# Four weight loads a unit: the first issue at 0.4 instead of 0.1 slots, the distance 0.4 instead of 0.25

## The chip, the cores and the metric

The kernel runs on one core of a Trainium2 chip. The metric is the device time of one execution in microseconds (us); a kernel's time is the median of several executions. The profile is that of one execution, with its own time beside it.

## The reference

The kernel computes one encoder block for 2048 positions of width 1024. An RMS norm and one wide input projection give the queries, keys and values of 14 attention pieces, two gates' inputs and the merge gates. Attention looks at windows of neighbours (piece A, and three dilated groups of piece B with dilation 1, 4 and 16), the outputs are gated, projected and added to the input:

```python
h = rms_norm(x, norm_gain[layer])
proj = h @ w_in[layer]
qa, ka, va, qb, kb, vb, ga, gb, mg = jnp.split(proj, split_idx, axis=-1)
...
ya, _ = banded_attention(qa, ka, va, A_WINDOW, 1, rel_bias[:, :A_Q_HEADS], sink_a[layer])
ya = ya.reshape(bsz, S, A_WIDTH) * jax.nn.silu(ga)
...
    o, l = dilated_group(qb[:, :, g], kb[:, :, g], vb[:, :, g], window, dilation,
                         rel_bias[:, c0:c0 + B_HEADS_PER_GROUP])
...
yb = yb.reshape(bsz, S, B_WIDTH) * jax.nn.silu(gb)
br_a = ya @ w_branch_a[layer]
br_b = yb @ w_branch_b[layer]
...
merged = gates[:, :, 0] * br_a + gates[:, :, 1] * br_b
x = x + merged @ w_out[layer]
```

## The kernel before

**Numbers in two halves.** TensorE multiplies 16-bit numbers. Each float32 operand is therefore split into a high and a low f16 part, and a product takes three matmuls. The normed input stands in SBUF as `XH` and `XL`, transposed. The weights of a unit are loaded as float32 (`wraw`), multiplied by the norm's gain, squared and summed for a scale, and then split into `wh` and `wl`.

**Units and slots.** The attention pieces are 14 units (`UNITS`): piece A twice, and piece B in four head pairs times three groups `g`, in the order g = 1, 2, 0 for each head pair. A unit has eight slots, and a slot projects two blocks of 128 rows: two times 24 matmuls of line 709 with 384 columns. Slots can also hold "fills", products for the gates (line 333). After the units come four slots with fills alone, and then the gates, branches and output projection. The stretch with the units runs from about 70 to 1380 us.

**An order written by hand.** `at(t, f)` puts a step on a heap with its planned time in slots, and `until` emits what is due between two matmuls. This fixes the order of the instructions on each engine and on SyncE's DMA queue (SP). It fixes no time: on the chip each engine runs its list as fast as its waits allow. Planned times below are in slots from the first slot of a unit.

**What one slot makes.** The two projections are copied out of PSUM (`evac_qk`, `v_hi`, `v_lo`), queries and keys are normed and split (`square` to `swap`, on ScalarE, VectorE and GpSimd), and `turn` (line 794) issues two DMA transposes `kq<-spl` on SP. They are planned 1.118 slots behind the end of the slot's projections (`NORM`). An attention item then takes its logits (line 879, reads `kq`), and its probabilities are turned by a DMA transpose `pt<-p` (line 917) and multiplied with the values (line 928). Items are planned on a grid of half a slot for piece B: the first of a slot has its logits 2.887 slots behind the slot's start (`LS`), its `pt` 0.525 behind the logits and its values 1.829 behind them (`LAGS`, `LV`).

**The weights.** The tile `wraw` exists once. In unit u the weights of unit u + 1 are loaded, in four quarters of 384 KB (256 KB for the two weights behind the units). The loop below plans the four loads, the gains (`w_gain`, line 193, GpSimd), the squares, and the splits. In the last two slots of most units the same tile holds other weights, which are read for the last time by a split that is planned at 7.942. The steps of one `chain` keep their order among themselves.

```python
def w_load(u, parts=(0, 1, 2, 3)):
...
    for i in parts:
        nc.sync.dma_start(out=raw[:, 2 * i:2 * i + 2, :n], in_=src[:, 2 * i:2 * i + 2, :])
...
for u in range(NU + 1):
    t = 8 * u
    steps = [(t + W_STEP[0] + B_GAP[0] * i, w_load, u + 1, (i,)) for i in range(4)]
    for i in range(4):
        steps += [(t + W_STEP[2] - W_STEP[6] + W_STEP[3] * i, w_gain, u + 1, i),
```

With the values before, the loads are planned at 0.1, 0.35, 0.6 and 0.85 slots, and the gains at 1.558, 2.003, 2.448 and 2.893. The first eight slots prepare unit 1; the loads for unit 0 have planned times of their own. The loop has 15 rounds, so 60 loads.

Of the kernel before, what the change touches and what calls it, by code (L numbers as in the profile page):

```python
# [75 lines left out]
Y_DMA = (-0.097, 0.45, 0.55, 1.05, 1.13, 1.2, 1.25)  # L76
Y_MAX_DMA = (0.026, 1.4, 1.45)
GATE = (-0.123, -0.064, 0.329)
W_STEP = (0.1, 0.465, 1.9, 0.445, 4.197, 0.146, 0.342)
W_MAX = (3.762, 3.892)  # L80
G_PREP = (5.907, 6.882, 7.102, 7.671, 7.712, 7.812, 7.942)
N_PREP = (6.3, 7.15, 7.753)
B_GAP = (0.25, 0.138, 0.231)
Y_FREE = 0.15
Y_MAX = (0.026, 0.815, 0.839)
Y_MAX_A = (0.026, 0.88, 0.904)
# [37 lines left out]
def block_kernel(tc, x, w_units, w_gate, w_mrg, w_brn, w_out, w_bra, gain, qkg, sink, bias_a, bias_b, b_merge, out):  # L124
# [215 lines left out]
    def g_load(c, raw=None, parts=(0, 1)):  # L340
        if c not in gw:
            if raw is None:
                raw = sp0.tile([128, NCH, 128], F32, name="graw", bufs=2)[:]
            gw[c] = [raw]
        raw = gw[c][0]
        for i in parts:
            nc.sync.dma_start(out=raw[:, 4 * i:4 * i + 4, :], in_=w_gate[c][:, 4 * i:4 * i + 4, :])
# [76 lines left out]
    def at(t, f, *args):  # L424
        seq[0] += 1
        heapq.heappush(heap, (t, seq[0], f, args))
# [8 lines left out]
    def chain(steps):  # L435

        steps = sorted(steps, key=lambda e: e[0])
        done = [0]

        def go(k):  # L440
            if done[0] < k or steps[k][1](*steps[k][2:]) is False:
                at(now[0] + .04, go, k)
            else:
                done[0] = k + 1

        for k, e in enumerate(steps):
            at(e[0], go, k)
# [715 lines left out]
# [5 lines that stand above are left out]
                      (t + W_STEP[2] + W_STEP[3] * i, w_square, u + 1, i),  # L1168
                      (t + W_STEP[4] + W_STEP[3] * i, w_hi, u + 1, i),
                      (t + W_STEP[4] + W_STEP[5] + W_STEP[3] * i, w_lo, u + 1, i)]  # L1170
        chain(steps + [(t + d, f, u + 1) for d, f in zip(W_MAX, (w_sum, w_pow))])

    for c, u, slots in FILLS:
# [6 lines left out]
        for i in range(2):  # L1180
            at(t + G_PREP[0] + B_GAP[1] * i, lambda u=u, c=c, i=i: g_load(c, pre[u][0], (i,)))
        chain([(t + G_PREP[1] + .1 * i, g_gain, c, i) for i in range(2)]
              + [(t + d, f, c) for d, f in zip(G_PREP[2:], (g_square, g_sum, g_pow, g_hi, g_lo))])
    for k in range(8):
# [4 lines left out]
        for j in range(4):  # L1189
            at(t + N_PREP[0] + B_GAP[2] * j, piece_load, u, k, j)  # L1190
        for half in range(2):
# [662 lines left out]
```

## Time and profile before

| | us |
|---|---|
| median of three executions | 1915.26 |
| lowest and highest of them | 1915.14, 1917.81 |
| the profiled execution | 1916.12 |
| span of its profile | 1914.3 |

The span runs from the first to the last instruction of the profile; some 1.8 us of the execution's time lie around it. In the profile PE is TensorE, DVE VectorE, ACT ScalarE, POOL GpSimd and SP the DMA queue of SyncE. A line such as "PE s L879 <- DMA kq<-spl: 2.9, 4, 1.0" says that TensorE, before the matmuls of line 879 into the tile `s`, sat idle for 2.9 us in all, in 4 places, at most 1.0 us in one, until the DMA that writes `kq` from `spl` had landed. Matmuls overlap in the pipeline: one of 384 columns is shown with 0.33 us, and the next one starts 0.16 us behind it.

### The profile page before, as it was taken

To read this page: it belongs to the slowest core of one execution; us is meant where nothing else is said; L and a number is where in the kernel's file an instruction comes from. 1 tells how busy PE (TensorE), PEld (TensorE's weight loads), DVE (VectorE), ACT (ScalarE), POOL (GpSimd) and SP (SyncE) were. 2 spreads that over 40 slices of the span, in tenths; PEclk is the share of its full clock that TensorE was granted. 3 is DMA by queue.
4 is the path that set the end of the run, shared out by engine and by line. 5 is a ranking of instruction groups with operands and counts; after the bars stand their busy time and mean duration, and the time that the engine had idled before them with its cause. 6 is when DMAs were issued, how large, how long until landed. Compare 5 with 4: busy or idle time off the path is not lost.

```text
span 1914.3 us, 39281 instructions
## 1 busy us (share of the span) xinstructions
PE 1899.4 (99%) x13578; PEld 1190.4 (62%) x13578; DVE 1360.3 (71%) x3522; ACT 1120.4 (59%) x2496; POOL 843.7 (44%) x1848
## 2 busy tenths in 40 slices
PE   8999999999999999999999999999999999999999
PEld 6566666677666688566787667876544444444444
DVE  8578886887767877577776877768686667767312
ACT  8468776787656776566766767666544545323100
POOL 4333454344545655446555565555412211223543
DMA  8459986897968697578768788766822346778763
GB/s 285 128 107 181 194 166 152 149 199 151 189 104 197 131 186 139 116 158 175 168 123 155 160 174 150 130 118 132 186 75 99 105 154 220 223 245 261 265 226 138
DMA packets 624585, 316.56 MB, mean 165 GB/s; under 512 B 492928, under 2 KB 562176, under 8 KB 623104
## 3 DMA queue, kind: packets, MB, share of 16 engines
q1 hardware_dynamic: 605952, 305.39, 69.2%
q10 hardware_dynamic: 18432, 8.66, 2.0%
q8 instruction: 106, 1.74, 0.4%
q14 instruction: 95, 0.78, 0.2%
HBM read 129.91 MB, written 65.27 MB: 102 GB/s over the span
## 4 chain that ended last, share of the span: by engine, by line
PE 86%; DVE 5%; DMA 3%; POOL 2%; issue 2%; ACT 2%; SPq 0%; DVEq 0%; POOLq 0%; ACTq 0%
PE pj L709 37%; PE pj L333 15%; PE fps L333 11%; PE fps L1721 6%; PE s L879 5%; PE pv L928 4%; PE fps L1516 3%; DMA kq<-spl 2%; PE pj L1721 2%; PE pj L609 2%; PE pj L1516 1%; DVE p L911 1%; DVE pr L894 1%; DVE qss L753 1%; DVE rw L765 0%
## 5 line engine op out<-in xcount | busy, mean ns | idle before, releaser
L709 PE MATMUL pj<-wh,XL 128*128 128x384 f16 x1792 | 586.1, 327 | 0.0
L709 PE MATMUL pj<-wh,XH 128*128 128x384 f16 x1792 | 584.5, 326 | 1.4 <-DVE vt L741 1.4
L709 PE MATMUL pj<-wl,XH 128*128 128x384 f16 x1792 | 584.7, 326 | 0.0
L709 PEld LDWEIGHTS <-XH 128*128 128x128 f16 x3584 | 410.5, 116 | 151.9 <-issue 1.7
L894 DVE CUSTOM_DVE_ANT_0 pr<-s,b,ubuf 128x256 f32<-128x256 f32 (+3 forms) x512 | 219.1, 465 | 81.1 <-PE s L879 79.3
L709 PEld LDWEIGHTS <-XL 128*128 128x128 f16 x1792 | 207.7, 116 | 70.3 <-issue 1.2
L911 DVE SCALAR_TENSOR_TENSOR p<-pr,p 128x512 f16<-128x512 f32 (+2 forms) x256 | 189.5, 740 | 20.2 <-ACT p L907 20.0
L786 POOL COPY spl<-spl 128x256 f16<-128x256 f16 (+1 forms) x224 | 88.1, 423 | 185.7 <-DVE spl L781 184.3
L726 ACT ACTIVATE rw<-pj 128x256 f32<-128x256 f32 (+1 forms) x224 | 86.8, 388 | 138.3 <-PE pj L709 124.2
L907 ACT ACTIVATE p<-pr 128x512 f16<-128x512 f32 (+2 forms) x256 | 159.2, 622 | 6.2
L333 PEld LDWEIGHTS <-wh 128*128 128x128 f16 x960 | 93.7, 98 | 110.5
L879 PE MATMUL s<-kq 128*128 128x256 f16 (+3 forms) x1168 | 147.8, 254 | 2.9 <-DMA kq<-spl 2.9
L928 PEld LDWEIGHTS <-pt 128*128 128x128 f16 x3024 | 125.4, 97 | 34.8
L286 POOL TENSOR_TENSOR rs_t<-rs_y 128x8 f32<-128x8 f32 (+1 forms) x112 | 40.2, 359 | 238.4 <-DVE rs_y L278 189.6
L771 POOL TENSOR_TENSOR rw<-rw,g 128x256 f32<-128x256 f32 (+1 forms) x112 | 90.8, 811 | 109.9 <-DVE rw L765 76.1
L193 POOL TENSOR_TENSOR wraw<-wraw,gn 128x768 f32<-128x768 f32 (+1 forms) x80 | 112.5, 1411 | 55.5 <-DMA wraw<-in_w_mrg_dram 43.6
L928 PE MATMUL pv<-vt,pt 128*128 128x65 f16 (+1 forms) x3024 | 132.7, 192 | 0.0
L879 PEld LDWEIGHTS <-kq 128*128 128x128 f16 x1184 | 101.5, 98 | 45.5 <-DMA kq<-spl 4.4
L765 DVE TENSOR_TENSOR rw<-rw,qr 128x512 f32<-128x512 f32 (+1 forms) x112 | 103.6, 925 | 30.8 <-POOL qr L295 29.9
L741 DVE SCALAR_TENSOR_TENSOR vt<-pj,vt 128x128 f16<-128x128 f32 (+1 forms) x224 | 62.1, 277 | 88.3 <-ACT vt L735 87.4
L333 PE MATMUL pj<-XH,gh 128*128 128x512 f16 x320 | 121.3, 379 | 0.0
L333 PE MATMUL pj<-XH,gl 128*128 128x512 f16 x320 | 121.2, 379 | 0.0
(281 smaller groups left out, 3799.0 us busy)
## 6 DMA issues: line engine op xcount, KB each, us to landing
wraw<-in_w_units_dram SPq DMA_DIRECT2D x56, 384.0 KB, 4.8
mtd<-mm SPq DMA_DIRECT2D x56, 256.0 KB, 3.7
M<-mtd SPq DMA_DIRECT2D x8, 1792.0 KB, 9.5
mgd<-fg SPq DMA_DIRECT2D x39, 256.0 KB, 2.1
zd<-z ACTq DMA_DIRECT2D x128, 66.0 KB, 2.6
zz<-zd SPq DMA_DIRECT2D x64, 132.0 KB, 2.8
xt<-in_x_dram SPq DMA_DIRECT2D x16, 512.0 KB, 9.4
gtd<-yo SPq DMA_DIRECT2D x32, 256.0 KB, 2.9
```

The lines of the kernel that those rows point to most:

```text
L193: G.tensor_tensor(v, v, gn[:, c0:c0 + 2].unsqueeze(2).to_broadcast([128, 2, n]), OP.mult)
L333: out.append(lambda w=w, xx=xx, ch=ch, i=i: T.matmul(ps[:], lhsT=w[:, ch, c0:c0 + 128], rhs=xx[:, ch, ts], start=(i == 0), stop=(i == n - 1)))
L709: out.append(lambda lhs=lhs, rhs=rhs, ch=ch, k=k: T.matmul(ps[:, :384], lhsT=lhs[:, ch, :], rhs=rhs[:, ch, :], start=(k == 0), stop=(k == ...
L765: V.tensor_tensor(q, q, self.rr[:, :n].unsqueeze(2).to_broadcast([128, n, HD]), OP.mult)
L771: G.tensor_tensor(k, k, GT[un.br][:].unsqueeze(1).unsqueeze(1).to_broadcast([128, 2, un.nk, HD]), OP.mult)
L786: G.tensor_copy(sp[:, i, nh:, :, :], sp[:, i, nq:nh, ::-1, :])
L879: T.matmul(self.sv[j][:, o:o + k1 - k0], lhsT=q[:, h, qo:qo + 128], rhs=kt[:, un.nq + kh + v * un.nk, k0:k1], start=(v == 0), stop=(v == 1))
L894: V.tensor_tensor_reduce(out=self.pv[:, j, self.p0:self.p0 + W], in0=self.sv[j], in1=un.bias[:, self.h0 + j, self.b0:self.b0 + W], scale=I ...
L907: A.activation(self.sp[:, :128 * n], self.pr, AF.Copy, scale=PSC)
L911: V.scalar_tensor_tensor(self.sp[:, 128 * n:], self.pr, PSC, self.sp[:, :128 * n], OP.mult, OP.subtract)
L928: T.matmul(self.po[:, j, :w], lhsT=p[:, n * j + s, :], rhs=un.v[key][:, vh, c0:c0 + w], start=(k == 0 and s == 0), stop=(k == 2 and s == n ...
L1721: mm.append(lambda ch=ch, k=k, w=w, i=i: T.matmul(ps[:, :cols.stop - cols.start], lhsT=m[:, a, ch, k, :], rhs=wt[w][:, b, ch, cols], start ...
```

## The change

Two numbers of the plan change. `W_STEP[0]` is the planned time of the first load, `B_GAP[0]` the distance of the four. Both are used nowhere else.

```diff
@@ -76,11 +76,11 @@
 Y_DMA = (-0.097, 0.45, 0.55, 1.05, 1.13, 1.2, 1.25)
 Y_MAX_DMA = (0.026, 1.4, 1.45)
 GATE = (-0.123, -0.064, 0.329)
-W_STEP = (0.1, 0.465, 1.9, 0.445, 4.197, 0.146, 0.342)
+W_STEP = (0.4, 0.465, 1.9, 0.445, 4.197, 0.146, 0.342)
 W_MAX = (3.762, 3.892)
 G_PREP = (5.907, 6.882, 7.102, 7.671, 7.712, 7.812, 7.942)
 N_PREP = (6.3, 7.15, 7.753)
-B_GAP = (0.25, 0.138, 0.231)
+B_GAP = (0.4, 0.138, 0.231)
 Y_FREE = 0.15
 Y_MAX = (0.026, 0.815, 0.839)
 Y_MAX_A = (0.026, 0.88, 0.904)
```

The loads of a unit are now planned at 0.4, 0.8, 1.2 and 1.6 slots. No instruction is added or removed, and no other step's planned time changes.

## The prediction, on record before the changed kernel ran

> **What bounds the kernel now.** The page's first lines come first: which engine has no idle time, and how much is left.
>
> ```profile
> span 1914.3 us, 39281 instructions
> PE 1899.4 (99%) x13578; PEld 1190.4 (62%) x13578; DVE 1360.3 (71%) x3522; ACT 1120.4 (59%) x2496; POOL 843.7 (44%) x1848
> ```
>
> TensorE is the bound, and 14.9 us of its span are idle. The stretches say where: the units run from 70 to 1380 us, the rest is behind them.
>
> ```profile
> core 0: us, PE busy (x) PEld busy (x) DVE busy (x) ACT busy (x) POOL busy (x), PEclk, DMA share, GB/s
> 70.00:1380.00 1310.00, 1304.54 (x10680) 906.74 (x10679) 988.17 (x2841) 882.00 (x2100) 674.73 (x1715) 1.00 0.78 155
> 1380.00:1914.00 534.00, 531.20 (x2492) 242.55 (x2490) 315.33 (x529) 185.12 (x301) 141.33 (x109) 1.00 0.55 182
> ```
>
> The 60 loads that move are issued in the first stretch. TensorE is idle there for 1310 - 1304.54 = 5.5 us, at a granted clock of 1.00. No schedule of DMAs can win much more than that. The list of what TensorE waited for in that stretch, next, names the whole of it:
>
> ```profile
> PE s L879 <- DMA kq<-spl: 2.9, 4, 1.0
> PE pj L709 <- DVE vt L741: 1.4, 1, 1.4
> PE pt L210 <- DVE yo L1023: 0.8, 2, 0.4
> PE pt L210 <- DVE wm L217: 0.4, 1, 0.4
> ```
>
> Over half of it, 2.9 us in four places, ends with the landing of a `kq` transpose. Nothing waits for `pt`, and nothing on TensorE for a weight. The timeline of TensorE shows three of the four places; the row before each wait is the last matmul that was issued.
>
> ```profile
> 703.39 0.33 PE L709 MATMUL pj<-wh,XH 128*128 128x384 f16 x1
> 704.28 0.61 PE L879 MATMUL s<-kq 128*128 128x256 f16 x4 [0.56 <-DMA kq<-spl]
> ...
> 964.52 0.33 PE L709 MATMUL pj<-wh,XL 128*128 128x384 f16 x1
> 964.68 0.33 PE L709 MATMUL pj<-wh,XH 128*128 128x384 f16 x1
> 965.96 0.61 PE L879 MATMUL s<-kq 128*128 128x256 f16 x4 [0.95 <-DMA kq<-spl]
> ...
> 1207.12 0.33 PE L709 MATMUL pj<-wh,XH 128*128 128x384 f16 x1
> 1208.48 0.61 PE L879 MATMUL s<-kq 128*128 128x256 f16 x4 [1.03 <-DMA kq<-spl]
> ```
>
> Without a wait the next matmul starts 0.16 us behind the last (964.52 to 964.68). The starts are 0.89, 1.28 and 1.36 us apart, so the waits cost 0.73 + 1.12 + 1.20 = 3.05 us of issue, more than the idle times shown. These are the same place in units 6, 9 and 12: the last pair of slots' `kq` of a g = 1 unit, due at 1.118 in the next unit, for logits due at 1.887.
>
> Why does `kq` land late there? SP's queue in unit 9, then all `kq` transposes of the run, then those of 956 to 967 us:
>
> ```profile
> 950.18 0.40 SPq L188 DMA_DIRECT2D wraw<-in_w_units_dram  x1
> 950.67 2.57 SPq L794 DMA_TRANSPOSE kq<-spl  x2
> 953.29 0.62 SPq L188 DMA_DIRECT2D wraw<-in_w_units_dram  x1
> 954.08 1.23 SPq L917 DMA_TRANSPOSE pt<-p  x1
> 955.37 1.06 SPq L188 DMA_DIRECT2D wraw<-in_w_units_dram  x2
> 957.22 1.23 SPq L917 DMA_TRANSPOSE pt<-p  x1
> 959.32 3.31 SPq L794 DMA_TRANSPOSE kq<-spl  x2
> 962.73 4.48 SPq L917 DMA_TRANSPOSE pt<-p  x2
> ```
>
> ```profile
> L794 SPq DMA_TRANSPOSE kq<-spl x224: 1209/1237/3433, 89.9 to 1354.5; - x112
> ...
> DMA to landing us min/median/max: 2.7/3.2/7.5
> ```
>
> ```profile
> L794 SPq DMA_TRANSPOSE kq<-spl x2: 1341/1608/1876, 959.3 to 960.8; - x2
> ...
> DMA to landing us min/median/max: 5.6/6.1/6.6
> ```
>
> The median from issue to landing is 3.2 us; the first of the late pair takes 6.6 and lands at 959.32 + 6.6 = 965.9, just when the logits start. All four loads of the unit were issued in the nine microseconds in front of it. The DMA engines, in the same stretch:
>
> ```profile
> 950.00:955.00 5.00, 5.00 (x45) 4.40 (x44) 4.33 (x20) 3.44 (x9) 3.33 (x13) 1.00 1.09 248
> 955.00:960.00 5.00, 5.00 (x44) 4.45 (x43) 4.54 (x14) 4.29 (x11) 1.69 (x5) 1.00 1.05 287
> 960.00:965.00 5.00, 5.00 (x43) 4.14 (x41) 3.38 (x8) 2.35 (x7) 3.84 (x11) 1.00 1.24 131
> ```
>
> The share before the last number is over 1 in each row: the DMA engines have no gap, and `kq` stands in line.
>
> **The change, part by part.** Nothing is added or removed: 60 loads of 256 or 384 KB, 60 issues on SP of about half a microsecond (0.40, 0.62 and half of 1.06 above). What moves is their place on SP. By the planned times SP's order in a unit behind g = 1 is now: load 0.1, two `kq` 0.118, load 0.35, `pt` 0.412, loads 0.6 and 0.85, `pt` 0.912, two `kq` 1.118, `pt` 1.412 and 1.912, as the rows show. Afterwards it is: two `kq`, load 0.4, `pt` 0.412, load 0.8, `pt` 0.912, two `kq` 1.118, load 1.2, `pt` 1.412, load 1.6, `pt` 1.912. So load 0 takes the place of the old load 1 (953.3), load 1 that of the pair (955.4 or a little later), and loads 2 and 3 stand behind the critical `kq`, not in front of it.
>
> *The stalls (edit's gain).* A load of 384 KB is 0.393 MB, at 287 GB/s an estimated 1.37 us of the DMA engines. Two loads leave the line in front of the late `kq`; but the two that stay start 2 to 3 us later, so that less of them is done when `kq` is issued. Net, between one load and two leave the line: 1.37 to 2.74 us earlier. The stalls are 0.73, 1.12 and 1.20 us, all under the lower figure, the last by 0.17. I take all three as gone: -3.05 us. The ends are 0, if something else than these bytes holds `kq`, and -3.05. What is late next there is the matmul stream itself, since the logits stand in program order.
>
> *The fourth wait* comes behind the last unit.
>
> ```profile
> 1355.74 0.38 PE L333 MATMUL pj<-XH,wh 128*128 128x512 f16 x1
> 1355.95 0.38 PE L333 MATMUL pj<-XL,wh 128*128 128x512 f16 x1
> 1356.70 0.61 PE L879 MATMUL s<-kq 128*128 128x256 f16 x4 [0.37 <-DMA kq<-spl]
> ```
>
> ```profile
> DMA to landing us min/median/max: 2.8/3.1/3.5
> ```
>
> It costs 0.75 - 0.21 = 0.54 us, and its `kq` pair (last row) took 3.5 and 2.8 us to land, near the usual 3.2. Three loads stand close in front of it and would be fewer, but a `kq` of usual latency has little to win. I count 0; the ends are 0 and -0.54.
>
> *The gains that read the loads.* Each load is issued later: load 0 by 0.3 slots, load 3 by 0.75. What covers this is the time between landing and gain. In the stretch of the units the view of the tile `wraw` names no GpSimd row among those who waited for it, and has this for its loads' landing (first row); the other two rows are the tightest place.
>
> ```profile
> DMA to landing us min/median/max: 2.6/4.0/8.5
> ```
>
> ```profile
> 766.10 0.58 SPq L188 DMA_DIRECT2D wraw<-in_w_units_dram  x1
> ...
> 773.24 1.47 POOL L193 TENSOR_TENSOR wraw<-wraw,gn 128x768 f32<-128x768 f32 x1
> ```
>
> They belong to unit 8's weights: the old load 1 (new place of load 0) is issued at 766.10 and the first gain starts at 773.24. That leaves 7.1 us, against a median landing of 4.0. The cost is 0 while a load lands within 7.1 us. If the cover were gone, GpSimd would stand in the gain with the norms of the next `kq` queued behind it.
>
> *What is queued behind the moved loads on SP.* Load 2 delays `pt` 1.412, load 3 `pt` 1.912 by half a microsecond of issue and up to 1.37 us of transfer each.
>
> ```profile
> L917 SPq DMA_TRANSPOSE pt<-p x256: 1188/1247/2912, 108.2 to 1371.0; - x128
> ...
> DMA to landing us min/median/max: 2.4/3.7/8.4
> ```
>
> Before the change `pt` already took up to 8.4 us to land, and TensorE never waited for it: its values come 1.3 slots behind its issue. I take 0. The `kq` at 2.118, behind load 3, serve logits that the queue of items has pushed to 3.387 in the units behind g = 1, so 0 too; the ends for both are 0 and one stall of a size seen, 1.2 us.
>
> *Sum.* 0 - 3.05 + 0 + 0 = -3.05 us. The span is 1914.3 and the profiled execution 1916.12, with 1.8 us around the span that the change leaves alone; it would give 1913.1. The median of the runs, 1915.26, is 0.9 lower than that execution, and the same difference taken from it gives **1912.2 us**.
>
> **The rivals.**
>
> *It changes little* (1915, or up to 1 less). The bytes of the loads are not what holds `kq`. For it: from 960 to 965 the DMA share is at its highest, 1.24, with 131 GB/s, under half of the row above. The engines were occupied, yet little moved, while by SP's rows the last things issued were transposes; these may hold each other up with or without loads. Against it: the late `kq` are exactly those with four loads issued close in front.
>
> *It is slower: late gains.* Place: `w_gain` on GpSimd. It decides from a landing of over 7.1 us. Price: with the longest landing seen, 8.5 us, the gain waits 1.4 us; at every one of 15 rounds and passed on whole this is 21 us (1936). As most of it would be taken up by GpSimd's idle time (44% busy), I price it at a third, +7: 1922. The Trainium skill, "DMA: Bandwidth & Descriptors", section "Rules for kernel authors", speaks for this rival: issue a DMA early, compute, and wait for its semaphore late. By that rule alone the change gives up lead and wins nothing, and the result is 1915 to 1922. The trace bears it out only in part: no gain in the units waited for its load, so the lead is larger than used.
>
> *More goes than the three stalls.* The fourth wait (0.54) and the one for `vt` (1.4 + 0.16) go as well, the second because later steps shift: 3.05 + 0.54 + 1.56 = 5.15, 1910.1. For `vt` only chance speaks: its row names VectorE, not a DMA.
>
> **How the numbers follow.** A measurement of this kernel can tell about 0.2%, 3.8 us, from no change. Forecast: 0.60, of which 0.15 lie beyond 3.8 us (with the fourth wait and a little more). Little change: 0.20. Slower: 0.10. More: 0.10, of which 0.09 beyond 3.8 us. Faster is 0.15 + 0.09 = 0.24, slower 0.10, the same 0.66. The range reaches down to 1911.0, the forecast less the fourth wait and half of the `vt` wait. It reaches up to 1917.0: no change, and 1.7 us for one or two new stalls or for the spread of the runs before (up to 1917.81). It leaves out the slower rival and about half of the last one.
>
> **What would show each step.** Right: in units 6, 9 and 12 SP shows two loads in front of the second pair of `kq`, that pair lands in 3 to 5 us, and the waits list has `kq` with at most 0.5 us in one place. Wrong: `kq` still takes over 5.5 us there (the first rival); GpSimd waits for `wraw` between 70 and 1380 us (the second); or TensorE waits for `pt` or for a `kq` in a unit's third slot. A changed busy time of TensorE in the stretch behind 1380 us would mean that the change does something that I have not seen.

## The result, and the profile after

| | before | after |
|---|---|---|
| median of 20 executions, us | 1915.58 | 1912.71 |
| lowest and highest, us | 1913.88, 1920.87 | 1911.79, 1913.76 |
| profiled execution, us | 1916.12 | 1912.08 |
| span of its profile, us | 1914.3 | 1910.3 |

The ratio is 0.9982, with a 95% interval of 0.9977 to 0.9988: 2.9 us are gone. That is 0.15%, small, but clear of the interval with 20 executions of each. The executions also lie closer together than before. The two profiled executions differ by more, 4.0 us, because the one before lies 0.5 us above its median and the one after 0.6 below.

The page's first lines of the kernel after, then its row for the stretch with the units (columns as before: busy us and count of each engine, granted clock, DMA share, GB/s):

```profile
span 1910.3 us, 39284 instructions
PE 1899.4 (99%) x13578; PEld 1191.0 (62%) x13578; DVE 1360.1 (71%) x3522; ACT 1119.2 (59%) x2496; POOL 843.8 (44%) x1848
```

```profile
70.00:1380.00 1310.00, 1307.46 (x10701) 908.82 (x10700) 990.32 (x2847) 881.09 (x2100) 674.71 (x1715) 1.00 0.78 155
```

TensorE's busy time is the same 1899.4 us to the tenth, and every engine's count is the same; the three instructions more in the first line are semaphore instructions. The work did not change. In the stretch its idle time fell from 5.5 to 1310 - 1307.46 = 2.5 us, by the 2.9 us that stood beside `kq`. The list of what TensorE waited for in that stretch says so directly:

```profile
PE pj L709 <- DVE vt L741: 1.4, 1, 1.4
PE pt L210 <- DVE yo L1023: 0.8, 2, 0.4
PE pt L210 <- DVE wm L217: 0.4, 1, 0.4
```

The other three rows stand as they were, and the `kq` row is missing. What happened on SP in unit 9 (start, duration, what), and how long that pair then took to land:

```profile
949.23 2.56 SPq L794 DMA_TRANSPOSE kq<-spl  x2
951.84 0.57 SPq L188 DMA_DIRECT2D wraw<-in_w_units_dram  x1
952.52 1.24 SPq L917 DMA_TRANSPOSE pt<-p  x1
953.80 0.58 SPq L188 DMA_DIRECT2D wraw<-in_w_units_dram  x1
955.80 1.24 SPq L917 DMA_TRANSPOSE pt<-p  x1
957.90 2.61 SPq L794 DMA_TRANSPOSE kq<-spl  x2
960.57 0.88 SPq L188 DMA_DIRECT2D wraw<-in_w_units_dram  x1
961.55 1.24 SPq L917 DMA_TRANSPOSE pt<-p  x1
962.84 0.57 SPq L188 DMA_DIRECT2D wraw<-in_w_units_dram  x1
```

```profile
L794 SPq DMA_TRANSPOSE kq<-spl x2: 1212/1260/1308, 957.9 to 959.2; - x2
DMA to landing us min/median/max: 4.0/4.3/4.7
```

Two loads stand in front of the second pair and two behind it. The pair landed after 4.7 us at most, where it had taken 6.6. TensorE's timeline at the same logits has no wait:

```profile
963.32 0.33 PE L709 MATMUL pj<-wh,XL 128*128 128x384 f16 x1
963.48 0.33 PE L709 MATMUL pj<-wh,XH 128*128 128x384 f16 x1
963.64 0.60 PE L879 MATMUL s<-kq 128*128 128x256 f16 x4
```

The matmuls start 0.16 us apart, logits included, where 1.28 us had passed. The stretches of the DMA engines:

```profile
950.00:955.00 5.00, 5.00 (x45) 4.46 (x43) 4.31 (x19) 3.16 (x9) 3.20 (x12) 1.00 0.99 216
955.00:960.00 5.00, 5.00 (x45) 4.42 (x44) 4.67 (x15) 3.08 (x8) 2.06 (x8) 1.00 1.04 219
960.00:965.00 5.00, 5.00 (x43) 4.42 (x42) 3.65 (x8) 3.08 (x8) 3.81 (x9) 1.00 1.19 204
```

Packets still take about all of the engines' time (0.99 to 1.19), and 204 to 219 GB/s are moved evenly. Before the change the rate was 287 and then 131 GB/s. The last rows of the two do not hold the same transfers: from 960 to 965 us two loads are issued after the change (960.57 and 962.84) and none before it, where the last was issued at 956. So the step from 131 to 204 GB/s does not show that transposes move faster.

### The profile page after: what moved, and what is told of

It is laid out like the page before. It is cut to its first block, busy times and chain, and to the rows that moved or that the text cites. A ratio compares the mean times of both kernels' runs of the same rounds, so it can differ in the third digit from the quotient of the medians.

```text
span 1910.3 us, 39284 instructions
## 1 busy us (share of the span) xinstructions
PE 1899.4 (99%) x13578; PEld 1191.0 (62%) x13578; DVE 1360.1 (71%) x3522; ACT 1119.2 (59%) x2496; POOL 843.8 (44%) x1848
## 4 chain that ended last, share of the span: by engine, by line
PE 92%; DVE 3%; POOL 2%; issue 1%; ACT 1%; DMA 1%; SPq 0%; DVEq 0%; POOLq 0%; ACTq 0%
PE pj L709 41%; PE pj L333 16%; PE fps L333 11%; PE fps L1721 6%; PE s L879 5%; PE pv L928 4%; PE fps L1516 3%; PE pj L1721 2%; PE pj L609 2%; PE pj L1516 1%; DVE p L911 0%; DVE qss L753 0%; DVE pr L894 0%; ACT jk L481 0%; DVE spl L781 0%
```

## The experiments

Eight kernels ran, four with each set of runs of the kernel before. Ratios are to those runs (median 1915.70 us for the first four, 1915.48 for the others), and edits are against the changed kernel. The theory: `kq` is late in units 6, 9 and 12 because of the bytes of the loads in line in front of it. The rivals: that the distance of the loads counts, or their start; that the gain is spread over all units; and that the transposes hold each other up whatever the loads do.

### One number alone

The start alone, loads planned at 0.4, 0.65, 0.9 and 1.15:

```diff
-B_GAP = (0.4, 0.138, 0.231)
+B_GAP = (0.25, 0.138, 0.231)
```

> First load at 0.4 slots, distance as before (0.25): planned 0.4, 0.65, 0.9, 1.15. Only load 3 stands behind the kq pair due at 1.118. Theory (the bytes of the loads in line in front of that kq make it late in units 6, 9 and 12): one load less in front brings kq earlier by half of what the two loads of the change brought (there 0.8, 1.9 and 2.2 us), so 0.4, 1.0 and 1.1 us against stalls of 0.73, 1.12 and 1.20: about 0.3, 0.2 and 0.1 us are left, TensorE's wait for kq falls from 2.9 to at most 0.7 us, time 1913.0 to 1913.6. Rival (the distance of the loads is what counts, because transposes and loads that overlap slow each other down): waits stay over 2 us, time about 1915.

Measured: 1913.79 us, 0.9990 (0.9981 to 0.9999). The distance alone, loads at 0.1, 0.5, 0.9 and 1.3:

```diff
-W_STEP = (0.4, 0.465, 1.9, 0.445, 4.197, 0.146, 0.342)
+W_STEP = (0.1, 0.465, 1.9, 0.445, 4.197, 0.146, 0.342)
```

> First load at 0.1 slots as before, distance 0.4: planned 0.1, 0.5, 0.9, 1.3. Again only load 3 stands behind the kq pair due at 1.118, but loads 1 and 2 stay close in front of it. Theory: one load less in front, as with the start alone: TensorE's wait for kq at most 0.9 us, time 1913.0 to 1913.8. Rival (only the later start counts, because it takes the first load away from in front of the kq pair due at 0.118): waits stay near 2.9 us, time about 1915.5.

Measured: 1912.30 us, 0.9985 (0.9976 to 0.9993). The waits of TensorE for `kq` with the start alone; with the distance alone there is no such row:

```profile
PE s L879 <- DMA kq<-spl: 0.6, 1, 0.6
```

This one wait stands at 1353.8 us, behind the last unit. In units 6, 9 and 12 either number alone ends the waits, and either one puts load 3 behind the pair and leaves three in front. Both rivals fall. That the start alone came out somewhat slower than expected (1913.0 to 1913.6) is within the intervals of these runs.

### Where the gain is made

The new plan in units 6, 9 and 12 alone, and then in all units but these:

```diff
-    steps = [(t + W_STEP[0] + B_GAP[0] * i, w_load, u + 1, (i,)) for i in range(4)]
+    steps = [(t + (0.4 + 0.4 * i if u in (6, 9, 12) else 0.1 + 0.25 * i), w_load, u + 1, (i,)) for i in range(4)]
```

> The new plan of the loads in units 6, 9 and 12 alone, the old plan in the others. Theory (all of the gain but the last half microsecond comes from one kq pair in each of these three units): the three waits are gone, the one behind the last unit (0.4 us idle) stays, time 1912.5 to 1913.3. Rival (the gain is spread over all units by many small delays): less than a third of the gain, time over 1914.6.

Measured: 1913.26 us, 0.9987 (0.9978 to 0.9996).

```diff
-    steps = [(t + W_STEP[0] + B_GAP[0] * i, w_load, u + 1, (i,)) for i in range(4)]
+    steps = [(t + (0.1 + 0.25 * i if u in (6, 9, 12) else 0.4 + 0.4 * i), w_load, u + 1, (i,)) for i in range(4)]
```

> The counterpart: the old plan in units 6, 9 and 12, the new one in all others. Theory: the three waits of 0.6 to 1.0 us stay, only the one behind the last unit may go, time 1914.8 to 1915.6. Rival (the gain is spread over all units): time under 1914.

Measured: 1916.29 us, 1.0000 (0.9991 to 1.0009), 0.7 us above the expected range and within the interval. The waits for `kq`, first of the kernel with three units moved, then of the one with the others moved (us in total, places, longest):

```profile
PE s L879 <- DMA kq<-spl: 0.6, 1, 0.6
```

```profile
PE s L879 <- DMA kq<-spl: 4.4, 4, 2.0
```

Three of 15 rounds carry the gain, and the other twelve none that can be told with these intervals of 1.7 us either way. The last wait (behind the last unit) stays in the first. In the second, the same three places cost more than before the change (longest 2.0 against 1.0), although the plan of these units is that of before. Whether that is the other units' new plan or chance, one profile does not tell. The times scatter too: this kernel's executions lie between 1912.99 and 1918.31 us, those of the change itself, run beside the next three, between 1911.71 and 1913.51.

### Four loads in front again

The plan of the change, but in units 6, 9 and 12 loads 2 and 3 go back in front of the pair:

```diff
-    steps = [(t + W_STEP[0] + B_GAP[0] * i, w_load, u + 1, (i,)) for i in range(4)]
+    steps = [(t + ((0.4, 0.8, 0.9, 0.905)[i] if u in (6, 9, 12) else 0.4 + 0.4 * i), w_load, u + 1, (i,)) for i in range(4)]
```

> The changed kernel, with loads 2 and 3 moved in units 6, 9 and 12 alone to 0.9 and 0.905, so that all four loads are in front of the kq pair due at 1.118 and later than before the change. Theory (bytes in line): kq in these units lands later by two loads' worth, by the change's own numbers 0.8 to 2.2 us and by transfer time up to 2.7 us; the three waits come back with 2.5 to 6.3 us together, time 1915.2 to 1919.0. Rival (transposes hold each other up with or without loads): time as the changed kernel, 1912.7.

> The changed kernel itself, beside the next three on the same chip: 1912.7 us, no wait of TensorE for kq.

Measured: 1915.73 us, 1.0000 (0.9991 to 1.0009), beside the changed kernel with 1912.54 us, 0.9985 (0.9976 to 0.9994). The whole gain is given back, at the lower end of what was expected. First its waits for `kq`, then the landing of the pair in unit 9:

```profile
PE s L879 <- DMA kq<-spl: 3.2, 3, 1.7
```

```profile
L794 SPq DMA_TRANSPOSE kq<-spl x2: 1348/1626/1903, 960.4 to 961.8; - x2
DMA to landing us min/median/max: 5.7/6.1/6.6
```

The first two loads stand as in the change, the number in front is that of before, and the landing is that of before (5.6/6.1/6.6); in units 6 and 12 the longest is 7.3 and 7.7 us. Only loads 2 and 3 of three units differ from the changed kernel, so these loads cause the three waits, and the rival that the transposes are late without them falls.

### All four behind, and the gains late

```diff
-    steps = [(t + W_STEP[0] + B_GAP[0] * i, w_load, u + 1, (i,)) for i in range(4)]
+    steps = [(t + 1.13 + 0.14 * i, w_load, u + 1, (i,)) for i in range(4)]
```

> All four loads behind the kq pair: planned 1.13, 1.27, 1.41 and 1.55 in every unit. Theory: no load is in line in front of that kq, so its waits stay away; but the first gain, planned at 1.558, is now issued before its load has landed: GpSimd waits 2 to 4 us for wraw in most units with short slots, 20 to 40 us in all. Most of that is taken from GpSimd's idle time and from the slack of the next kq: 1912.5 to 1917. Rival (late gains are passed on to TensorE whole): 1930 or more.

Measured: 1918.28 us, 1.0014 (1.0005 to 1.0023), some 5.7 us slower than the changed kernel beside it and 1.3 above the expected range, but far under the rival's 1930. What GpSimd waited for, of the tile `wraw`, and then what TensorE waited for:

```profile
POOL wraw L193 <- DMA wraw<-in_w_units_dram: 35.9, 10, 6.3
POOL wraw L193 <- DMA wraw<-in_w_mrg_dram: 6.4, 2, 3.9
```

```profile
PE pj L709 <- DVE vt L741: 4.6, 4, 2.6
PE pt L1000 <- DVE ya L1118: 1.2, 1, 1.2
PE pt L210 <- DVE yo L1023: 0.8, 2, 0.4
PE pv L928 <- DMA pt<-p: 0.7, 1, 0.7
PE pt L210 <- DVE wm L217: 0.4, 1, 0.4
```

There is no `kq` row. GpSimd stood 42 us in front of gains. TensorE has 3.2 (`vt`) + 1.2 + 0.7 = 5.1 us of waits more than in the changed kernel, an eighth at most. The chain of work leads from the wait back to a late gain for 3.2 us of them: three waits for `vt` (0.6, 1.1 and 0.4 us) and the 1.2 for `ya`. The rows name VectorE: its `v_lo` (line 741) frees a projection's bank, and it stands in one list with steps that wait for late work. The 0.7 us stand behind a `pt` transpose that took 5.4 us to land, and the rest, at 1101 us, behind the split of the next section. The landing of the pair in units 6, 9 and 12, with no load in front of it:

```profile
DMA to landing us min/median/max: 2.8/3.5/4.2
...
DMA to landing us min/median/max: 4.3/4.7/5.1
...
DMA to landing us min/median/max: 2.8/3.3/3.7
```

The changed kernel, with two loads in front, has 5.3, 4.7 and 5.3 us as the longest in the same places. Without the two the pair lands earlier in two of three units, and no earlier in unit 9.

### A further wait

The largest wait left, for `vt`, is no matter of the loads. VectorE in the changed kernel:

```profile
1094.24 1.28 DVE L386 SCALAR_TENSOR_TENSOR gl<-wraw,ubuf,gh 128x1024 f16<-128x1024 f32 x1
1095.43 0.69 DVE L781 TENSOR_TENSOR spl<-rw,spl 128x512 f16<-128x512 f32 x1
1096.03 0.29 DVE L741 SCALAR_TENSOR_TENSOR vt<-pj,vt 128x128 f16<-128x128 f32 x1
```

The split into `gl` goes first, and `v_lo` (line 741), which frees the bank, queues behind it with one other step. Moved behind both:

```diff
-G_PREP = (5.907, 6.882, 7.102, 7.671, 7.712, 7.812, 7.942)
+G_PREP = (5.907, 6.882, 7.102, 7.671, 7.712, 7.812, 8.11)
```

> The changed kernel, with the last split of the other weights (gl, planned at 7.942) moved to 8.11, behind the v_lo that TensorE waits for at 1094.7 us. Theory (that wait of 1.4 us is VectorE being in gl, 1.28 us, when the projections' bank is to be freed): the wait is gone or under 0.3 us, time 1911.2. Rival (v_lo is late for another reason, or the fill that reads gl now waits for it): 1912.7 or more.

Measured: 1911.19 us, 0.9980 (0.9971 to 0.9989), against 1912.54 for the changed kernel beside it. The wait shrank as expected:

```profile
PE pj L709 <- DVE vt L741: 0.2, 1, 0.2
```

This is the fastest version, below both kernels. Its interval and that of the changed kernel, both taken against the kernel before, overlap. But eight of its eleven executions lie below the fastest of the changed kernel's (1911.71 us), and the medians differ by 1.35 us, about the 1.2 us that the wait lost.

## Why the prediction was right, step by step

*The bound* was TensorE with 5.5 us of waits in the stretch, and only the `kq` waits moved. Right: the other rows are unchanged.

*The three stalls.* Predicted -3.05 us; measured 1912.71 - 1915.58 = -2.87. Moving three units alone brought 2.4 us of it (1913.26 against 1915.70), and putting loads back there took it all away. The sizes were right place by place: both traces hold the same 13578 matmuls in the same order, and matched one by one the changed kernel wins 0.73, 1.13 and 1.21 us at the three places (forecast 0.73, 1.12 and 1.20). Of the profiles' 4.0 us, 0.45 were won ahead of the first load that moves and owe nothing to the change. Of the 0.5 us between the forecast 1912.2 and the measured 1912.71, 0.3 is the median before, which was 1915.26 with three executions and 1915.58 with 20.

*How much earlier `kq` lands.* The working had 1.37 to 2.74 us. In unit 9 the pair's longest landing went from 6.6 to 4.7, by 1.9. In units 6 and 12 it is:

```profile
DMA to landing us min/median/max: 6.0/6.1/6.2
...
DMA to landing us min/median/max: 5.0/6.3/7.5
```

```profile
DMA to landing us min/median/max: 4.6/4.9/5.3
...
DMA to landing us min/median/max: 4.8/5.0/5.3
```

Before is the first fence, after the second: 0.9 and 2.2 us earlier. The term was mis-sized in unit 6, where 0.9 is under the range; that stall was only 0.73, so it went all the same, with some luck. Its sign of being right was a landing in 3 to 5 us. The longest landing held to that in unit 9 alone; 5.3 in the other two lies between that and the 5.5 that would have been wrong.

*The picture of a line of bytes* held in that loads in front make the pair late, but a load counts by what is left of it when the pair is issued, not by standing in front. These are the landings of the last loads in front in unit 9, before (loads 2 and 3) and after (load 1):

```profile
DMA to landing us min/median/max: 5.7/6.0/6.2
```

```profile
DMA to landing us min/median/max: 4.2/4.2/4.2
```

Before, the last load lands at 955.98 + 6.2 = 962.2, 2.9 us behind the pair's issue (959.32), and the first two have landed by then. After, load 1 lands at 953.80 + 4.2 = 958.0, 0.1 us behind it (957.90). "The DMA engines have no gap" was read into a share over 1. From 963 to 964 us the share is 1.09 while 13 GB/s are moved, so it does not mean that data flow all the time. What the prediction did not see in that stretch is told in the last section.

*The fourth wait* was counted at 0, with 0.54 as its other end. This term was mis-sized: the wait went in both profiles of the changed kernel, and in the matched matmuls 0.46 us are won there. The pair that was thought to have little to win landed in 3.1 us instead of 3.5. The wait stands on an edge: with the old plan in the last round or the start alone it stayed (0.4 to 0.6 us idle), and with the new one it came back once with 0.2 us, in the kernel with the other units moved. The medians, with 2.87 us, show less than the four places together (3.5), and why is open.

*The gains.* GpSimd never waited for a load in the changed kernel's units. The tightest place is this one, SP and then GpSimd:

```profile
764.17 0.47 SPq L188 DMA_DIRECT2D wraw<-in_w_units_dram  x1
```

```profile
772.04 1.47 POOL L193 TENSOR_TENSOR wraw<-wraw,gn 128x768 f32<-128x768 f32 x1
```

7.9 us lie between them, where 7.1 were predicted.

*The slower rival* was a true mechanism that did not set in at 0.4 slots. At 1.13 slots it did, and its pass-through was an eighth at most, not the third of the prediction's price. The Trainium skill ("DMA: Bandwidth & Descriptors", "Rules for kernel authors") asks to issue a DMA early. The trace agrees for these loads at 1.13 slots, where gains waited 42 us, and disagrees between 0.1 and 0.4, where later was better by 2.9 us.

*The first rival* (little change) had read the 131 GB/s as transposes that hold each other up. The time and the run with four loads in front decide against it as far as the waits go: without the loads they are gone. That little moves there for a while is real, and the last section has what stands beside it.

## What to carry to other kernels

On a queue whose transfers are issued in a fixed order, a bulk load with slack should not stand close in front of a small transfer that the bottleneck engine waits for: what is left of it at that moment delays the small one. List each transfer's time from landing to use, and move the loads with much of it behind those with none, as long as they still land before their own reader. A plan that repeats in 15 rounds can have its whole effect in three of them, so look for the places where a wait ends, not for the average.

## What was not expected of the hardware

Something beside the loads stands at all three late pairs. The page lists a DMA queue with packets of the kind `instruction`, 16 KB each (first row). One starts at 962.50 us in the kernel before, and the other two rows show the DMA engines around it:

```profile
q8 instruction: 106, 1.74, 0.4%
```

```profile
962.00:963.00 1.00, 1.00 (x9) 0.88 (x7) 0.29 (x1) 0.92 (x4) 0.74 (x4) 1.00 1.78 271
963.00:964.00 1.00, 1.00 (x17) 0.90 (x16) 0.63 (x1) 0.79 (x2) 0.92 (x3) 1.00 1.09 13
```

It is so in general: in the trace's packets between 70 and 1380 us there are 84 of these, and the other packets move 163 GB/s on average in the microsecond ahead of one, and 75 from 0.5 to 1.5 us behind its start. So the 131 GB/s stand in part beside such a packet. Of the `kq` transposes that were issued with no load into `wraw` under way, 17 had such a packet start in the 2 us behind their issue and landed in 4.25 us (median); the other 146 landed in 2.82.

Loads and packets together fit the three of 15 rounds that have the waits. For the first transpose of the pair behind the loads, us to landing:

| | no such packet in its flight | one such packet |
|---|---|---|
| no load under way | 2.8 to 3.1 (before, units 0, 3, 4, 5, 11) | 4.2, 5.1, 3.7 (all four behind, units 6, 9, 12) |
| two loads under way | 4.8, 3.8, 4.5, 2.8 (before, units 7, 8, 10, 13) | 6.2, 6.6, 7.5 (before, units 6, 9, 12) |

The three late pairs are the only ones of the 15 rounds with both. It also fits that unit 9 lands in 5.1 us with no load in front. That the loads delay the pairs is shown by the runs. That these packets do is not shown: no run moves them, and a pair that is late for another reason meets a packet more easily.

The change also narrowed the executions from 7.0 us between lowest and highest to 2.0, which was not forecast. Its cause is not shown.
